# A macaron layer on one Trainium2 core: another order of work in the mixer, mean squares by wide products, inverse roots by log, exp and a Newton step

## The chip, the cores and the metric

The kernel runs on one core of a Trainium2 chip. The metric is device microseconds of one execution; the number for a kernel is the median of its runs. A profile is one further execution with every instruction and DMA recorded. Engines are named as in the profile: PE is TensorE (PEld its weight loads), DVE is VectorE, ACT is ScalarE, POOL is GpSimd and SP is SyncE, which issues most DMAs.

## The reference

One layer of a streaming encoder on x (512 tokens by 1024 features, float32):

```
x = x + 0.5 * swiglu(rms(x), ffn1)          # 1024 -> 2816 -> 1024
h = rms(x);  q, k, v, u = h @ w_in          # 512 columns each
a = attention(rms(q), rms(k), v)            # 8 heads of 64, a bias by clipped distance
p = for each window 2, 4, 8, 16: (trailing mean of u - u) @ pool_w * pool_scale
x = x + concat(a, p) @ w_out
x = x + 0.5 * swiglu(rms(x), ffn2)
x = rms(x)
```

rms divides by the square root of the mean square plus 1e-6 and multiplies by a gain. q and k are normed for each token and head.

## The kernel before, in words

All large products are float32 at full precision, made from three products of a high and a low part: `mm3` (L198, L199, L200) issues high by high, low by high or high by low, and the last of the three, each 128 by 128 by 512 or by 256. The parts of a weight are made on the way: SP loads 512 KB, ACT casts the high part (L132, in the mixer L1117), DVE subtracts for the low part (L133, in the mixer L1122). `mm3` reads its moving operand in an order that alternates between the two halves of the row (`p (a i) -> p i a`, a = 2), and the engines that read a PSUM tile put it back with the views `ordered` and `natural`.

The two feed-forward blocks (roughly the first 335 us and the last 310 us of the span) use a seven-product scheme of block sums. POOL makes the sums of the down weights in DRAM: `Down.make_sums` copies one element of a tile named after it (`mark`, so that POOL waits for it) and then issues DMAs that copy or add whole weight rows (L715, L717). For the second block half of those 48 steps are issued in the mixer, as jobs `for i in range(LATE, LATE + EARLY)`: one job for each of the weight chunks 12 to 19, which holds that chunk's buffer until POOL has read it. The other half follows inside the second up-projection.

The three norms `n1`, `n2`, `n3` work with features on partitions, so the mean over features runs across partitions. ACT squares, DVE adds the squares of the eight feature tiles into `acc`. Then, in `per_token` (L319, for n2 L1151), four float32 products of `acc` with a column of ones give a sum per token; ACT takes the root and loads another function table; DVE makes the inverse root with a reciprocal and one Newton step (`rsqrt_of`) and a diagonal block; PE multiplies a block of ones with the diagonals (`spread`, L340, for n2 L1182: one float32 product of 512 columns), so that the value of each token stands on all partitions; ACT copies this to `rb` (L342). In a feed-forward block the first four PSUM banks can't be reused before DVE has read them with `rb` (L424).

The mixer (about 335 to 490 us) is a list of jobs, each with an engine, a cost, a rank and the buffers that it takes and frees. `plan()` orders them on paper, always taking the job of least rank whose inputs and buffers are ready on its own clock, and the instructions are recorded in that order; each engine then runs its list in order. The weight chunks are 4 for the first half of q and k, 4 for v, 4 for the second half, 4 for u, then 8 of the output projection. For each half of q and k: `evacuate` scales the projected tile by the norm `r` on ACT (L1312), ACT squares it (L1318), DVE reduces, `inverse` makes 32 inverse roots per token on DVE alone with an integer first guess and three Newton steps, DVE scales, PE transposes (L1356), ACT and DVE split the result (L1263, L1267). For each pair of heads PE makes the scores (L1516, 64 rows for each head, two heads at once in the two halves of the array); DVE adds the bias and takes the largest (L1524); ACT takes exp (L1532) and divides by the sum (L1543). For each head PE transposes the probabilities (L1580), ACT and DVE split them (L1589, L1594), `multiply` takes the product with v (L1605, 8 products of 512, 512, 384, 384, 128, 128, 256 and 256 columns), and ACT and DVE split its result (L1612, L1615, L1621). The four pooling groups run beside it, sums on POOL (L1430), and end in the map products (operands `m,wp`). The output products follow, then `add_out` on x (L1670).

Of the kernel before, what the change touches and what calls it, by code (L numbers as in the profile page):

```python
# [8 lines left out]
F32 = mybir.dt.float32  # L9
# [22 lines left out]
MAGIC = 1597463007.0  # L32
# [7 lines left out]
EARLY = 8  # L40
LATE = 12
# [4 lines left out]
    weights=(-1.0, 0.905, 3.0), qk=2.0, turn=1.015, head=0.9, pool=0.965, map=3.0, u=0.99,  # L46
    score=0.99, evac=0.3, bias=1.2, wp=1.5, add=0.935, next=0.965,
)
HOP = 0.45
SLOW = dict(act=1.06, dve=1.06)  # L50
# [6 lines left out]
def layer(  # L57
# [162 lines left out]
    ones = const.tile([P, P], F32, name="ones")  # L220
# [3 lines left out]
    nc.vector.memset(eps, EPS)  # L224

    def tables(func, after):

        nc.scalar.activation(table, after, func, scale=0.0)


    tables(AF.Sqrt, ones[:, 0:1])
    idle = abank()
    for _ in range(8):
        nc.tensor.matmul(idle[:, :P], ones, ones, start=True, stop=True)
# [29 lines left out]

    def rsqrt(v, n):

        half = small.tile([P, n], F32, tag=f"rs{n}", name=name("half"), bufs=4)
        y = small.tile([P, n], F32, tag=f"rs{n}", name=name("y"), bufs=4)
        nc.vector.tensor_scalar(
            half.bitcast(I32), v.bitcast(I32), 1, None, op0=ALU.logical_shift_right  # L270
        )
        nc.vector.tensor_scalar(
            y.bitcast(I32), half.bitcast(I32), -1.0, MAGIC, op0=ALU.mult, op1=ALU.add
        )
        for _ in range(3):
            a = small.tile([P, n], F32, tag=f"rs{n}", name=name("a"), bufs=4)
            b = small.tile([P, n], F32, tag=f"rs{n}", name=name("b"), bufs=4)
            z = small.tile([P, n], F32, tag=f"rs{n}", name=name("z"), bufs=4)
            nc.vector.tensor_tensor(a, y, y, op=ALU.mult)
            nc.vector.scalar_tensor_tensor(b, a, -0.5, v, op0=ALU.mult, op1=ALU.mult)  # L280
            nc.vector.scalar_tensor_tensor(z, b, 1.5, y, op0=ALU.add, op1=ALU.mult)
            y = z
        return y
# [10 lines left out]
    class Norm:  # L294
# [22 lines left out]
        def per_token(self, total, after=None):  # L317
            for t in range(NT):
                nc.tensor.matmul(  # L319
                    total[:, t : t + 1], self.acc[:, t * P : (t + 1) * P], ones[:, 0:1],  # L320
                    start=True, stop=True,
                )
            v, root, self.r = (
                small.tile([P, NT], F32, tag=what, name=name(what)) for what in ("v", "root", "r")
            )
            nc.scalar.activation(root, total[:, :NT], AF.Sqrt, scale=1.0 / D, bias=eps)
            if after:
                tables(after, root[:, 0:1])
            nc.vector.tensor_scalar(v, total[:, :NT], 1.0 / D, EPS, op0=ALU.mult, op1=ALU.add)
            rsqrt_of(v, root, self.r)  # L330
            self.diag = temp()
            nc.vector.tensor_tensor(
                self.diag.rearrange("p (t c) -> p t c", t=NT),
                ident.unsqueeze(1).to_broadcast([P, NT, P]),
                self.r.unsqueeze(2).to_broadcast([P, NT, P]),
                op=ALU.mult,
            )

        def spread(self, wide):
            nc.tensor.matmul(wide, ones, self.diag, start=True, stop=True)  # L340
            self.rb = small.tile([P, S], F32, tag="rb", name=name("rb"), bufs=1)
            nc.scalar.copy(self.rb, wide)  # L342

        def finish(self):
            self.per_token(abank(), AF.Silu)
            self.spread(abank())
# [309 lines left out]
    class Down:  # L656
# [14 lines left out]
        def __init__(self, order, pair, block, by_token, ahead=0):  # L671
# [11 lines left out]
            self.steps = sorted(  # L683
                (g + at + 2 * (i - T1), at, i, g)
                for i in self.terms for g in range(G) for at in range(2)
            )
# [124 lines left out]
        def product(self, acc, g, a, i, further=False, scale=None):  # L811
# [7 lines left out]
            if self.n_products == 12:  # L819
                tables(AF.Sqrt, a[0][:, 0, 0:1].bitcast(F32))  # L820
# [120 lines left out]
    with tc.tile_pool(name="mix", bufs=1, reuse_waits="tile") as mpool:  # L941
# [60 lines left out]
        def plan():  # L1002
# [30 lines left out]
            while len(order) < len(jobs):  # L1033
                moved = False
                for e in free:
# [97 lines left out]
        for i in range(LATE, LATE + EARLY):  # L1133
            job(
                "pool", 3.8, 5, lambda i=i: down2.make_sums(buf["part", i][0].bitcast(F32)),
# [13 lines left out]
        def per_token():  # L1149
            for t in range(NT):  # L1150
                nc.tensor.matmul(  # L1151
                    buf["total"][:, t : t + 1], n2.acc[:, t * P : (t + 1) * P], ones[:, 0:1],
                    start=True, stop=True,
                )

        n2_small = {}

        def root_of():
            for what in ("v", "root", "r"):
                n2_small[what] = small.tile([P, NT], F32, tag=what, name=name(what))  # L1160
            nc.scalar.activation(
# [885 lines left out]
```

## Time and profile before

| what | value |
|---|---|
| median of 3 runs | 810.72 us (810.51 to 812.14) |
| the profiled execution's own time | 809.87 us |
| its span, first to last instruction | 808.1 us |
| granted TensorE clock, mean | 0.998 |
| PE busy | 798.1 us (99%) |
| DVE busy | 712.2 us (88%) |
| ACT busy | 499.1 us (62%) |
| POOL busy | 144.8 us (18%) |
| moved by DMA | 158.56 MB, 196 GB/s |
| function tables loaded by ACT (L228) | 7, mean 1283 ns |

Busy time is the share in which an engine has an instruction in work. The ends of matmuls are modelled, so a full PE can hold small gaps; these show as the distance between the starts of two matmuls, which is what the prediction reads. A row of a timeline gives the start, the length, the engine, the line, the operation, out<-in with the tile's names, and shapes; in brackets stands the idle time before it and what ended that. A row of the waits gives who waited for whom, the sum, how often, and the longest. A row of the windows gives the busy time and count of each engine in that stretch, then the granted clock, the DMA share and GB/s.

### The profile page before, as it was taken

The numbers are of one execution on the slowest core, as the hardware profiler recorded it, in microseconds if no ns is written. First come the engines' busy times: TensorE is split into PE (matmuls) and PEld (weight loads), VectorE is DVE, ScalarE is ACT, GpSimd is POOL, SyncE is SP. The second block draws the span as 40 slices with busy tenths as digits, with TensorE's granted clock in tenths as the row PEclk, the third lists the DMA queues.
The fourth block names the chain that finished last, engine by engine and source line by source line (L and its number), as shares of the span: only waits on it lengthen the run. The fifth ranks groups of instructions, "written<-read, shape, count | busy, mean of one in ns | idle before, by whom it ended". The sixth has DMA issues, their size and how long they took to land.

```text
span 808.1 us, 14963 instructions
## 1 busy us (share of the span) xinstructions
PE 798.1 (99%) x5730; PEld 749.4 (93%) x5730; DVE 712.2 (88%) x1136; ACT 499.1 (62%) x854; POOL 144.8 (18%) x232
## 2 busy tenths in 40 slices
PE   9999999999999999999999999999999999999996
PEld 8889999999999999888888888899999999988986
DVE  7899999999996997778688798999989999996997
ACT  8446665556675765559649644465566665766584
POOL 0022222223220000100355354111111011100010
PEclk9999999999999999999999999999999999999999
DMA  8266889979999674431599767256766665869642
GB/s 291 74 209 209 235 226 248 205 194 253 249 291 313 218 215 159 133 119 50 146 256 247 192 209 198 85 116 193 181 175 171 169 182 148 254 238 329 218 143 105
DMA packets 73847, 158.56 MB, mean 196 GB/s; under 512 B 6560, under 2 KB 31664, under 8 KB 73392
## 3 DMA queue, kind: packets, MB, share of 16 engines
q1 hardware_dynamic: 49808, 109.09, 39.8%
q0 software_dynamic: 23680, 48.24, 28.4%
q8 instruction: 45, 0.74, 0.4%
q10 hardware_dynamic: 288, 0.27, 0.1%
q14 instruction: 26, 0.21, 0.1%
HBM read 153.38 MB, written 50.34 MB: 252 GB/s over the span
## 4 chain that ended last, share of the span: by engine, by line
PE 91%; DVE 4%; ACT 1%; issue 1%; ACTq 0%
PE mm L198 19%; PE mm L200 19%; PE mm L199 19%; PE a L199 10%; PE a L198 10%; PE a L200 10%; PE mm L1605 1%; PE mm L1516 1%; DVE aside L365 1%; PE a L1580 1%; PE mm L1580 1%; DVE aside L371 0%; PE a L1516 0%; DVE parts L133 0%; PE a L1605 0%
## 5 line engine op out<-in xcount | busy, mean ns | idle before, releaser
L571 ACT ACTIVATE t<-mm 128x256 f32<-128x256 f32 x105 | 40.5, 385 | 111.0 <-PE mm L200 109.1
L132 ACT CAST parts<-raw 128x1024 fp32r<-128x1024 f32 (+2 forms) x77 | 74.0, 968 | 54.8 <-PE mm L199 24.7
L133 DVE TENSOR_TENSOR parts<-raw,parts 128x1024 fp32r<-128x1024 f32 (+2 forms) x77 | 85.7, 1121 | 15.1 <-ACT parts L132 14.6
L199 PE MATMUL mm<-ha,parts 128*128 128x256 f32 x280 | 77.0, 275 | 0.0
L200 PE MATMUL mm<-ha,parts 128*128 128x256 f32 x280 | 77.0, 275 | 0.0
L198 PE MATMUL mm<-ha,parts 128*128 128x256 f32 x280 | 77.0, 275 | 0.0
L717 POOL DMA_DIRECT2D wsum<-in_wB_dram x72 | 71.0, 1123 | 26.0 <-DMA wsum<-wsum 14.2
L715 POOL COPY mark<-t 128x1 f32<-128x1 f32 x40 | 16.1, 403 | 331.0 <-DVE t L615 245.0
L482 DVE TENSOR_TENSOR parts<-wsum,parts 128x1024 fp32r<-128x1024 f32 x53 | 64.5, 1217 | 5.1 <-ACT parts L477 5.1
L477 ACT CAST parts<-wsum 128x1024 fp32r<-128x1024 f32 x53 | 53.8, 1047 | 0.7 <-PE mm L200 0.3
L198 PEld LDWEIGHTS mm<-ha,parts 128*128 128x128 f32 x280 | 53.8, 192 | 0.1
L199 PEld LDWEIGHTS mm<-ha,parts 128*128 128x128 f32 x280 | 53.8, 192 | 0.1
L200 PEld LDWEIGHTS mm<-ha,parts 128*128 128x128 f32 x280 | 53.8, 192 | 0.0
L198 PE MATMUL mm<-hhi,parts 128*128 128x512 f32 x128 | 49.5, 391 | 0.1
L200 PE MATMUL mm<-hhi,parts 128*128 128x512 f32 x128 | 48.7, 384 | 0.8 <-DVE parts L133 0.8
L133 DVE TENSOR_TENSOR ah<-acts,ah 128x512 fp32r<-128x512 f32 (+1 forms) x72 | 47.1, 661 | 2.6 <-ACT ah L132 2.5
L199 PE MATMUL mm<-hlo,parts 128*128 128x512 f32 x128 | 48.7, 382 | 0.0
L132 ACT CAST ah<-acts 128x512 fp32r<-128x512 f32 (+1 forms) x72 | 40.9, 580 | 8.8 <-PE mm L199 6.2
L482 DVE TENSOR_TENSOR parts<-raw,parts 128x512 fp32r<-128x512 f32 (+1 forms) x52 | 43.5, 857 | 0.6 <-ACT parts L477 0.6
L500 DVE TENSOR_TENSOR wsum<-raw 128x1024 f32<-128x1024 f32 x35 | 42.6, 1217 | 0.0
L477 ACT CAST parts<-raw 128x512 fp32r<-128x512 f32 (+1 forms) x52 | 39.3, 755 | 4.0 <-DMA raw<-in_wA_dram 3.5
L1122 DVE TENSOR_TENSOR parts<-raw,parts 128x1024 fp32r<-128x1024 f32 x24 | 30.3, 1265 | 11.4 <-ACT parts L1117 11.4
(344 smaller groups left out, 3059.8 us busy)
## 6 DMA issues: line engine op xcount, KB each, us to landing
raw<-in_wA_dram SPq DMA_DIRECT2D x87, 512.0 KB, 5.1
wsum<-in_wB_dram POOLq DMA_DIRECT2D x60, 512.0 KB, 7.4
raw<-wsum SPq DMA_DIRECT2D x36, 512.0 KB, 4.8
raw<-in_wB_dram SPq DMA_DIRECT2D x30, 512.0 KB, 4.8
wsum<-wsum POOLq DMA_DIRECT2D x20, 512.0 KB, 5.1
x<-in_xT_dram SPq DMA_DIRECT2D x16, 256.0 KB, 6.1
raw<-in_wQK_dram SPq DMA_DIRECT2D x8, 512.0 KB, 3.5
wsum<-in_wB_dram POOLq DMA_DIRECT2D x12, 256.0 KB, 5.4
```

What stands on the lines that cost most here:

```text
L132: nc.scalar.copy(hi, src)
L133: nc.vector.tensor_tensor(lo, src, hi.bitcast(F32), op=ALU.subtract)
L198: nc.tensor.matmul(acc, a[0], high, start=start, stop=False, **more)
L199: nc.tensor.matmul(acc, a[0], low, start=False, stop=False, **more)
L200: nc.tensor.matmul(acc, a[1], high, start=False, stop=stop, **more)
L477: nc.scalar.copy(hi, src)
L482: nc.vector.tensor_tensor(lo, src, hi.bitcast(F32), op=ALU.subtract)
L500: nc.vector.tensor_tensor(z, raw[:, : 2 * S], raw[:, S : 3 * S], op=ALU.add)
L571: nc.scalar.activation(natural(dst), ordered(src), AF.Copy, scale=scale)
L717: nc.gpsimd.dma_start(self.rows(i, g), self.rows(self.terms[i][at], g), **(dict(accum_op=ALU.add) if at else {}),)
L1122: nc.vector.tensor_tensor(lo, buf["raw", i], hi.bitcast(F32), op=ALU.subtract)
L1580: nc.tensor.transpose(buf["tp", h, group][:, n : n + P], buf["p", h, t][:, j * P : (j + 1) * P], ident,)
```

## The change

It has four parts.

**Norms.** The block of ones becomes a block of 1/1024. `acc` is multiplied by it in one wide product, so the mean stands on all partitions at once: for n1 and n3 as one float32 product of 512 columns, for n2 as two products on a high and a low part that ACT and DVE make first. ACT then takes log, exp with scale -0.5, and a square (`rough`), all from one function table, and DVE does one Newton step in two passes over 512 columns (`exact`). The four products with a column, the spread and its copy go. For n2, `r` per token is picked out of `rb` with the identity and a reduction. The inverse roots of q and k take log and exp on ACT (32 values each) and three passes on DVE in place of the integer guess and nine passes. The function tables loaded are 5 in place of 7.

**Product with v.** `multiply` reads its moving operand alternating between the halves of each block of 128 columns, and the three readers of the result go through views that undo this.

**Order in the mixer.** Ranks and costs of the planner change, and with them the order on every engine.

**Sums.** The mixer's 24 steps of weight sums become 16 jobs on chunks 4 to 19, and their sequence is by kind: first all copies of a kind, then all additions to them.

The diff, cut:

```diff
-EARLY = 8
-LATE = 12
+EARLY = 16
+LATE = 4
...
-    score=0.99, evac=0.3, bias=1.2, wp=1.5, add=0.935, next=0.965,
+    score=0.5, evac=0.3, bias=1.2, wp=1.1, add=1.1, next=0.965,
...
-SLOW = dict(act=1.06, dve=1.06)
+SLOW = dict(act=1.1, dve=1.06)
...
-    nc.vector.memset(ones, 1.0)
+    nc.vector.memset(mean_of.bitcast(F32), 1.0 / D)
...
+        def mean(self, wide, pair):
+            wide = wide.rearrange("p (i a) -> p i a", a=2)
+            for i in range(2):
                 nc.tensor.matmul(
-                    total[:, t : t + 1], self.acc[:, t * P : (t + 1) * P], ones[:, 0:1],
-                    start=True, stop=True,
+                    wide, mean_of, pair[i].rearrange("p (a i) -> p i a", a=2),
+                    start=i == 0, stop=i == 1,
+                )
+        def rough(self, wide, y, y2):
+            nc.scalar.activation(natural(y), ordered(wide), AF.Ln, bias=eps)
+            nc.scalar.activation(y, y, AF.Exp, scale=-0.5, bias=less_ln2)
+            nc.scalar.activation(y2, y, AF.Square, scale=2.0)
+        def exact(self, wide, y, y2):
+            nc.vector.scalar_tensor_tensor(
+                natural(y2), ordered(wide), EPS, natural(y2), op0=ALU.add, op1=ALU.mult
             )
+            self.rb = small.tile([P, S], F32, tag="rb", name=name("rb"), bufs=1)
+            nc.vector.scalar_tensor_tensor(
+                self.rb, y2, 3.0, y, op0=ALU.subtract, op1=ALU.mult, reverse0=True
             )
...
         def finish(self):
-            self.per_token(abank(), AF.Silu)
-            self.spread(abank())
+            wide, y, y2 = abank(), temp(), temp()
+            nc.tensor.matmul(
+                wide.rearrange("p (i a) -> p i a", a=2), mean_of.bitcast(F32),
+                self.acc.rearrange("p (a i) -> p i a", a=2), start=True, stop=True,
+            )
+            self.rough(wide, y, y2)
+            tables(AF.Silu, y[:, 0:1])
+            self.exact(wide, y, y2)
...
+            if ahead:
+                self.steps = [
+                    (0, at, i, g) for i in (T1, T3, T2, T4) for at in range(2) for g in range(G)
+                ]
...
-                        cost, scoring = cost + 0.1 * (score != scoring), score
+                        cost, scoring = cost + 0.2 * (score != scoring), score
...
-                var["rs"] = rsqrt(z.rearrange("p t h -> p (t h)"), NT * 8).rearrange(
+            def rough():
+                nc.scalar.activation(flat("log"), flat("mean"), AF.Ln)
+                nc.scalar.activation(flat("y"), flat("log"), AF.Exp, scale=-0.5)
...
             def multiply():
-                o = buf["o", h]
+                o = buf["o", h].rearrange("p (b i a) -> p b i a", a=2, i=P // 2)
...
-                            o[:, j * P :], v[j][:, h, :, :],
-                            buf["pT", h, group][i][:, at : at + (NT - j) * P],
+                            o[:, j:], v[j][:, h, :, :],
+                            turned.rearrange("p (b a i) -> p b i a", a=2, i=P // 2),
...
-        job("act", 1.5, 6, lambda: tables(AF.Sqrt, ones[:, 0:1]), list(at_prob.values()))
```

Three places show how the order moves. The first is PE in the first feed-forward block, where the last feature tiles meet the first four banks; `acc` is the sum of squares, `hhi` and `hlo` are the parts of the scaled x. Before:

```order
L199 MATMUL mm_167<-hlo_275,parts 128x512
L319 MATMUL a_330<-ones,acc_191 128x1 x4
L200 MATMUL mm_167<-hhi_274,parts 128x512
L198 MATMUL mm_164<-hhi_309,whi_314 128x512
L199 MATMUL mm_164<-hlo_310,whi_314 128x512
L200 MATMUL mm_164<-hhi_309,wlo_315 128x512
```

And in the changed kernel:

```order
L199 MATMUL mm_172<-hlo_280,parts 128x512
L334 MATMUL a_335<-acc_196,mean_of 128x512
L200 MATMUL mm_172<-hhi_279,parts 128x512
L198 MATMUL mm_169<-hhi_314,whi_319 128x512
L199 MATMUL mm_169<-hlo_315,whi_319 128x512
L200 MATMUL mm_169<-hhi_314,wlo_320 128x512
```

One product of 512 columns stands where four of one column stood, and the spread, which stood 17 products further on, has no successor.

The second place is ACT around the first transposes of q and k: `t` are the projected and the squared tiles, `qk_sb` marks the split of the transposed ones, `prob` the exp of the scores. Before:

```order
L1312 ACTIVATE t_4473<-mm_4306,r_4390 128x512
L1318 ACTIVATE t_4480<-t_4473 128x512
L1117 CAST parts<-raw_4437 128x1024
L1117 CAST parts<-raw_4449 128x1024
L1263 ACTIVATE m_4574<-a_4559,qk_sb 128x512
L1263 ACTIVATE m_4584<-mm_4564,qk_sb 128x512
L1263 ACTIVATE m_4591<-mm_4569,qk_sb 128x512
L1263 ACTIVATE m_4598<-mm_4579,qk_sb 128x512
L1117 CAST parts<-raw_4541 128x1024
L1532 ACTIVATE prob_620_4636,sm_4637<-prob_620_4636,sm_4637 128x512
```

And in the changed kernel:

```order
L1311 ACTIVATE t_4496<-t_4471 128x512
L1116 CAST parts<-raw_4417 128x1024
L1116 CAST parts<-raw_4463 128x1024
L1340 ACTIVATE log_4521<-var_4510 128x32
L1341 ACTIVATE y_4522<-log_4521 128x32
L1116 CAST parts<-raw_4537 128x1024
L1256 ACTIVATE m_4593<-mm_4577,qk_sb 128x512
L1256 ACTIVATE m_4601<-mm_4582,qk_sb 128x512
L1256 ACTIVATE m_4608<-mm_4588,qk_sb 128x512
L1256 ACTIVATE m_4623<-mm_4596,qk_sb 128x512
L1116 CAST parts<-raw_4548 128x1024
L1544 ACTIVATE prob_607_4645,sm_4646<-prob_607_4645,sm_4646 128x512
```

Log and exp of the head norms stand behind two weight casts, and a third cast now stands ahead of the splits.

The third place is PE near the end of the heads: `prob` marks transposes of the probabilities, `pTw` the product with v, `m,wp` the map products, other `m` the output products. Before:

```order
L1580 MATMUL a_5672<-ident,prob_779_5407 128x128
L198 MATMUL mm_5683<-m_5604,wp_4378 128x512
L199 MATMUL mm_5683<-m_5605,wp_4378 128x512
L200 MATMUL mm_5683<-m_5604,wp_4379 128x512
L198 MATMUL mm_5697<-m_5611,wp_4378 128x512
L199 MATMUL mm_5697<-m_5612,wp_4378 128x512
L200 MATMUL mm_5697<-m_5611,wp_4379 128x512
L1580 MATMUL a_5705<-ident,prob_804_5510 128x128
L1580 MATMUL a_5705<-ident,prob_799_5486 128x128
L1605 MATMUL a_5717<-pTw_5691,v_4748 128x512
```

And in the changed kernel:

```order
L198 MATMUL mm_5620<-m_5704,parts 128x512
L199 MATMUL mm_5620<-m_5705,parts 128x512
L200 MATMUL mm_5620<-m_5704,parts 128x512
L1592 MATMUL a_5783<-ident,prob_787_5492 128x128
L1592 MATMUL a_5783<-ident,prob_782_5482 128x128
L198 MATMUL mm_5695<-m_5704,parts 128x512
L199 MATMUL mm_5695<-m_5705,parts 128x512
L200 MATMUL mm_5695<-m_5704,parts 128x512
L198 MATMUL a_5789<-m_5750,wp_4374 128x512
L199 MATMUL a_5789<-m_5751,wp_4374 128x512
L200 MATMUL a_5789<-m_5750,wp_4375 128x512
L1592 MATMUL mm_5797<-ident,prob_790_5510 128x128
```

Map products and transposes that stood back to back now have output products between them. Between the second set of transposes of q and k and the last product with v, PE has 132 products of 512 columns of projection, map and output in place of 102; behind the last product with v stand 129 in place of 150. In the whole mixer the scores stand in 8 separate runs in place of 7.

More of the change, by code (lines that the diff above doesn't have):

```diff
@@ L262, in extended @@
         return load, fill, store
[L265 to L283, printed above, removed]
     def rsqrt_of(v, root, out):
@@ L682, in __init__ @@
             self.loaded, self.then, self.made = {}, {}, []
[L683 to L686, printed above, removed]
+            if ahead:
+                self.steps = [
+                    (0, at, i, g) for i in (T1, T3, T2, T4) for at in range(2) for g in range(G)
+                ]
+            else:
+                self.steps = sorted(
+                    (g + at + 2 * (i - T1), at, i, g)
+                    for i in self.terms for g in range(G) for at in range(2)
+                )
             n = len(self.steps)
@@ L1146, in layer @@
             at_acc = job("dve", 0.65, -5, None, [sq, at_acc])
[L1149 to L1161, printed above, removed]
-                n2_small["root"], buf["total"][:, :NT], AF.Sqrt, scale=1.0 / D, bias=eps
-            )
-            tables(AF.Exp, n2_small["root"][:, 0:1])
@@ L1166, in reciprocal_root, with mean_high, mean_low @@
-        def reciprocal_root():
-            v, n2.r = n2_small["v"], n2_small["r"]
-            nc.vector.tensor_scalar(
-                v, buf["total"][:, :NT], 1.0 / D, EPS, op0=ALU.mult, op1=ALU.add
-            )
-            rsqrt_of(v, n2_small["root"], n2.r)
+        def mean_high():
+            nc.scalar.copy(buf["sum", 0], n2.acc)
+        def mean_low():
+            nc.vector.tensor_tensor(
+                buf["sum", 1], n2.acc, buf["sum", 0].bitcast(F32), op=ALU.subtract
+            )
@@ L1177, in diagonal @@
-                n2.r.unsqueeze(2).to_broadcast([P, NT, P]),
+                by_token(buf["y"]), by_token(n2.rb), ident.unsqueeze(1).to_broadcast([P, NT, P]),
                 op=ALU.mult,
             )
-        def spread():
-            nc.tensor.matmul(buf["wide"], ones, buf["diag"], start=True, stop=True)
-        def spread_copy():
-            n2.rb = small.tile([P, S], F32, tag="rb", name=name("rb"), bufs=1)
-            nc.scalar.copy(n2.rb, buf["wide"])
-        total = z = job("pe", 0.5, -1, per_token, [at_acc], [("bank", "total")])
@@ L1189, in layer, with reduced @@
-        z = job("act", 1.8, -1, root_of, [z])
-        at_r = job("dve", 0.8, -1, reciprocal_root, [z], uses=["total"])
-        z = job("dve", 0.65, -1, diagonal, [at_r], [("t", "diag")])
-        z = job("pe", 0.9, -1, spread, [z], [("bank", "wide")], ["diag"])
-        at_rb = job("act", 0.55, -1, spread_copy, [z], uses=["wide"])
+        def reduced():
+            n2.r = small.tile([P, NT], F32, name="r")
+            nc.vector.tensor_reduce(n2.r, by_token(buf["y"]), axis=AX.X, op=ALU.add)
@@ new lines, in layer @@
+        pair = [("sum", i) for i in range(2)]
+        z = job("act", 0.6, -1, mean_high, [at_acc], [("m", key) for key in pair])
+        z = job("dve", 0.65, -1, mean_low, [z])
+        total = z = job("pe", 0.45, -1, mean, [z], [("bank", "mean")], pair)
+        z = job("act", 1.8, -1, rough, [z], [("t", "y"), ("t", "y2")])
+        z = at_rb = job("dve", 1.3, -1, exact, [z], uses=["mean", "y2"])
+        z = job("dve", 0.65, -1, diagonal, [z])
+        at_r = job("dve", 0.65, -1, reduced, [z], uses=["y"])
@@ L1621, in out_low @@
                 nc.vector.tensor_tensor(
-                    buf[pair[1]][rows, :], buf["rest", h][rows, :], buf["o", h][HD:, :], op=ALU.add
+                    by_block(buf[pair[1]]), by_block(buf["rest", h]), result(1), op=ALU.add
                 )
```

86 lines of the change are left out of this document (51 added, 35 removed).

## The prediction

> **What bounds the kernel now.** I read the page first: engine totals and the chain that ended last.
>
> ```profile
> span 808.1 us, 14963 instructions
> PE 798.1 (99%) x5730; PEld 749.4 (93%) x5730; DVE 712.2 (88%) x1136; ACT 499.1 (62%) x854; POOL 144.8 (18%) x232
> PE 91%; DVE 4%; ACT 1%; issue 1%; ACTq 0%
> ```
>
> PE has something in work for all but 10 us of the span and carries 91% of the chain. So a microsecond is won only by taking work from PE, by making a product shorter, or by closing one of PE's gaps. The second view is the list of PE's waits: who held it, then sum, count and longest in microseconds.
>
> ```profile
> PE a L234 <- DVE eps L224: 1.1, 1, 1.1
> PE mm L200 <- DVE parts L133: 0.8, 1, 0.8
> PE mm L198 <- DVE m L1621: 0.6, 1, 0.6
> PE a L319 <- DVE acc L315: 0.4, 1, 0.4
> PE a L1605 <- DVE pTw L1594: 0.3, 1, 0.3
> ```
>
> The first is the start of the program and stays. The others lie in the first norm and in the mixer, where the change works. All come from DVE, so the third view is the windows around them: stretch, its length, then busy time (count) of PE, PEld, DVE, ACT, POOL, then clock, DMA share and GB/s.
>
> ```profile
> 26.00:52.00 26.00, 25.47 (x117) 21.56 (x115) 23.90 (x32) 10.36 (x13) 3.62 (x4) 1.00 0.26 87
> 425.00:440.00 15.00, 14.97 (x93) 13.09 (x90) 13.21 (x46) 15.00 (x42) 10.84 (x16) 1.00 0.98 230
> 440.00:450.00 10.00, 8.98 (x51) 7.00 (x50) 9.50 (x22) 9.15 (x23) 2.15 (x3) 1.00 0.50 163
> ```
>
> After the first norm DVE works 23.90 of 26 us and then makes PE wait. In the later heads ACT is busy for all 15 us of a stretch, and in the next 10 us PE has its largest hole of the mixer, 1.02 us. The granted clock is 1.00 throughout.
>
> **The change part by part.** For the rate of a product I take a run of full-precision products, and the second norm that follows it.
>
> ```profile
> 340.05 0.38 PE L200 MATMUL mm<-parts,hlo 128*128 128x512 f32 x1
> ...
> 341.99 0.38 PE L200 MATMUL mm<-parts,hlo 128*128 128x512 f32 x1
> 342.21 1.02 PE L1182 MATMUL a<-t,ones 128*128 128x512 f32 x2
> 342.67 0.78 PE L198 MATMUL mm<-parts,hhi 128*128 128x512 f32 x1
> 343.28 0.38 PE L199 MATMUL mm<-parts,hhi 128*128 128x512 f32 x1
> ```
>
> From 340.05 to 341.99 are nine products, 0.2155 us each; lengths overlap, so I count from start to start. From 342.21 to 343.28 stand the spread and one such product: 1.07 - 0.2155 = 0.86 us for a wide float32 product.
>
> The first norm (a row's bracket is the idle time before it, and what ended it):
>
> ```profile
> 21.83 1.05 PE L319 MATMUL a<-ones,acc 128*128 128x1 f32 x8 [0.40 <-DVE acc L315]
> 22.74 0.46 PE L200 MATMUL mm<-hhi,parts 128*128 128x512 f32 x1
> ...
> 27.55 0.59 ACT L342 COPY rb<-a 128x512 f32<-128x512 f32 x1 [2.86 <-PE a L340]
> 28.17 0.69 DVE L424 TENSOR_TENSOR t<-mm,rb 128x512 f32<-128x512 f32 x1 [2.10 <-ACT rb L342]
> ...
> 52.23 0.70 PE L200 MATMUL mm<-hhi,parts 128*128 128x512 f32 x2 [0.75 <-DVE parts L133]
> ```
>
> 1. *First norm.* The column products take 22.74 - 21.83 = 0.91 us and go; the spread, 0.86, is replaced by one product like it. That is -0.9. Then the way to `rb`: before, DVE takes up the first bank at 28.17, 5.4 us after the columns, having idled 2.10. Now follow three ACT passes of 512 elements and two on DVE. With the groups of ACT by form:
>
> ```profile
> L314 ACT ACTIVATE t<-x 128x512 f32<-128x512 f32 x14 | 8.1, 614 | 0.0
> L228 ACT ACT_TABLE_LOAD x7 | 9.0, 1283 | 1.3 <-PEq L2032 1.2
> ```
>
> At 0.61 for an ACT pass and 0.69 for a DVE pass that is 3 x 0.61 + 2 x 0.69 = 3.2 us, and 1.0 for the product (the length at 342.21): 4.2 after 21.83, so about 26.1 instead of 28.17. The 2.10 us in which DVE idled is the only idle time of any size in its 26:52 stretch, and the 0.75 us of PE at 52.23 is its late result. DVE gains about 2 and adds 1.4 us of passes but drops the small steps of the root; with 0.75 needed, I take the wait as gone. Together -1.7. Bounds: 0 if DVE is as late as before by as much as PE is now early, -2.1 if the 0.40 at 21.83 goes too.
>
> 2. *Second norm.* Columns 0.91 and spread 0.86 become two products on parts, 2 x 0.2155 = 0.43: -1.3. The parts cost ACT and DVE a pass each; this lies beside the projection, which does not need `r` until it is read out. If that cover failed, 1.3 would be lost again (0.61 + 0.69).
>
> 3. *Third norm.*
>
> ```profile
> 509.14 1.22 DVE L371 TENSOR_TENSOR aside<-aside 128x1024 f32<-128x1024 f32 x1
> 510.28 0.68 DVE L424 TENSOR_TENSOR t<-mm,rb 128x512 f32<-128x512 f32 x1
> 511.11 0.45 PE L198 MATMUL mm<-hhi,parts 128*128 128x512 f32 x1
> ```
>
> Again -0.9 of columns. But PE starts on the freed bank at 511.11, 0.83 after DVE began to read it (0.68 long): PE follows DVE here, and arriving 0.9 earlier it would wait. In the new order the read stands one pass of 1.22 earlier on DVE. I take half, -0.5; ends 0 and -0.9.
>
> 4. *Product with v, and the scores.*
>
> ```profile
> 360.79 0.38 PE L200 MATMUL a<-parts,hlo 128*128 128x512 f32 x1
> 361.10 0.50 PE L1516 MATMUL a<-m,m 64*128 64x512 f32 x1
> ...
> 361.99 0.48 PE L198 MATMUL mm<-parts,hhi 128*128 128x512 f32 x1
> 362.31 0.38 PE L199 MATMUL mm<-parts,hhi 128*128 128x512 f32 x1
> ...
> 379.90 1.15 PE L1605 MATMUL mm<-pTw,v 128*128 128x512 f32 x6
> ...
> 381.18 0.38 PE L198 MATMUL a<-parts,hhi 128*128 128x512 f32 x1
> ```
>
> One head's eight products have 2560 columns and take 381.18 - 379.90 = 1.28 us; at 0.2155 for 512 they would take 1.08. The full-precision products already read alternating between two halves and are the faster ones per column. If the read order were all of it, 8 heads gain 8 x 0.20 = 1.6; if none, 0. Part of the 0.20 must be the short products of 128 and 256 columns and their many changes of width, so I take -0.6. [...]
>
> A run of scores costs a switch on either side: 361.10 - 360.79 = 0.31 and 362.31 - 361.99 = 0.32 in place of 0.2155, 0.2 together. Eight runs in place of seven: +0.2. Runs and transposes among more products switch more often too; with one such switch I take +0.4, ends +0.2 and +0.5.
>
> 5. *PE's waits in the mixer.*
>
> ```profile
> 443.32 0.60 PE L1580 MATMUL a<-ident,prob 128*128 128x128 f32 x4
> 443.99 0.45 PE L198 MATMUL mm<-m,wp 128*128 128x512 f32 x1
> ...
> 445.43 0.46 PE L198 MATMUL mm<-m,wp 128*128 128x512 f32 x1 [0.56 <-DVE m L1621]
> ...
> 446.24 0.44 PE L1580 MATMUL a<-ident,prob 128*128 128x128 f32 x2
> 446.99 1.25 PE L1605 MATMUL a<-pTw,v 128*128 128x512 f32 x6 [0.32 <-DVE pTw L1594]
> ```
>
> From 443.32 to 446.99, 3.67 us, PE does six transposes of 128 columns and six map products: 6 x 0.2155 = 1.3, and about 0.5 for the transposes (0.3 at the same rate by columns, more for their switches), so about 1.85 is lost. It waits for DVE because map products and transposes stand close together. The new order puts output products between them: 30 more products of 512 columns (6.5 us) before the last product with v. I take two thirds, -1.2; ends +0.5 (the largest single wait here moves elsewhere) and -1.9.
>
> 6. *At nothing.* Two table loads of 1.28 us go from ACT, which PE does not wait for by the list. Log and exp of the head norms add ACT passes of 32 elements and take six from DVE; PE does projections meanwhile. If that cover is gone, that is the third rival. The sums are spread over 16 chunks on POOL, 18% busy, and hold a chunk's buffer longer; no wait of PE is on POOL.
>
> Sum: -1.7 - 1.3 - 0.5 - 0.6 + 0.4 - 1.2 = -4.9. The profiled execution took 809.87, so it would take 805.0; the median of the runs is 810.72, 0.85 above it. I forecast for the median 810.72 - 4.9 = **805.8**. About 0.2%, 1.6 us, is what a measurement of this kernel can tell from no change.
>
> **The rivals.** *DVE stays the bound after both norms* (13%). Where DVE is 92% busy, PE's saved columns turn into a longer wait at the same bank. For: PE already waits for DVE at 52.23 and follows it at 511.11. Against: the 2.10 us hole that DVE has before 28.17. Terms 1 and 3 go: -4.9 + 2.2 = -2.7, 808.0.
>
> *The order does not do what it is there for* (10%). The heads end when ACT ends, and ACT was busy 15.00 of 15 us; moving products cannot help, and the read order gains nothing. Terms 5 and the -0.6 go: -3.1, 807.6. Against it: in 440:450 ACT has 0.85 us to spare, and PE's named releaser is DVE.
>
> *ACT in order, slower* (7%). On ACT the weight casts wait for PE to free a buffer, and everything behind them waits too.
>
> ```profile
> 352.33 1.05 ACT L1117 CAST parts<-raw 128x1024 fp32r<-128x1024 f32 x1 [2.89 <-PE mm L200]
> ...
> 357.30 0.69 ACT L1263 ACTIVATE m<-a,qk_sb 128x512 fp32r<-128x512 f32 x1 [3.92 <-PE a L1356]
> ```
>
> Now log and exp of the head norms stand behind two such casts, and a further cast ahead of the first exps. If each half of q and k comes 2.89 + 1.05 = 3.9 us later and PE finds nothing else, 7.9 us stand against -3.7 (the sum without term 5): 814.9. It decides from the point at which about half of the 7.9 reaches PE. Against: ACT idled 3.92 us before the splits at 357.30, so it has that much room in the first half.
>
> *The alternating read is slow* (3%). If neighbouring reads 64 columns apart cost the products with v as much again, 8 x 1.28 = 10.2 stands where -0.6 did: 810.72 - 4.3 + 10.2 = 816.6. [...] Against: the alternating products take 0.42 ns a column, the straight ones 0.50.
>
> **How the numbers follow.** Forecast 67%, rivals 13, 10, 7 and 3. The forecast's own terms by their ends reach from -7.6 to -0.3; that all go one way is unlikely, so I take about two microseconds below and, where the second and third cases lie, over three above: 803.6 to 809.2. That leaves out the slow cases and a tail on either side. Faster by over 0.2% means below 809.1: the forecast, less some 4%, and the next two cases, 0.86; within 0.2%: 0.05; slower: the last two, less a little of the third, 0.09.
>
> **What would show it.** Right: the norm product of the first norm directly followed by products 0.2155 apart; DVE taking up the first bank near 26 with little idle time; no wait of PE near 51; a head's products with v near 1.2 us; PE's waits in the mixer under 1 us in sum; PE busy about 793. Wrong: idle time of ACT ahead of the first splits that ends with PE, and PE waiting for ACT at the transposes of q and k; a head's products at 1.28 or over; a new wait of PE on DVE in the first four banks of either feed-forward block; PE waiting for POOL's sums or a weight cast where chunks are held longer.

## The result, and the profile after

The changed kernel takes 804.54 us (median of 6 runs, 803.98 to 804.97) against 810.36 us for the kernel before (809.85 to 812.14). The ratio is 0.9925, with a 95% interval of 0.9913 to 0.9937: 0.75% faster. The forecast was 805.8. Its profiled execution took 804.50 us, 5.37 less than that of before; the forecast's sum was -4.9.

The page of the changed kernel: span, busy time of each engine, and the chain that ended last.

```profile
span 802.7 us, 14916 instructions
PE 793.5 (99%) x5706; PEld 745.4 (93%) x5706; DVE 709.3 (88%) x1112; ACT 499.7 (62%) x857; POOL 152.5 (19%) x240
PE 89%; DVE 5%; issue 1%; DMA 1%; ACT 1%; SPq 0%; DVEq 0%; ACTq 0%
```

Of the 5.4 us that the span lost, PE's busy time lost 4.6. The list of PE's waits in the changed kernel:

```profile
PE a L242 <- DVE less_ln L226: 1.1, 1, 1.1
PE mm L200 <- DVE parts L133: 0.5, 1, 0.5
PE a L334 <- DVE acc L305: 0.4, 1, 0.4
PE mm L198 <- DVE t L418: 0.3, 1, 0.3
PE mm L198 <- ACT hhi L135: 0.2, 1, 0.2
```

The waits of the mixer are gone from the list. The one behind the first norm has shrunk from 0.8 to 0.5, and one at the first bank of the second feed-forward block (`t`, L418) is new. The windows show the same (stretch, length, then PE, PEld, DVE, ACT, POOL, clock, DMA share, GB/s); the change moved the mixer's work by 2.6 to 5.3 us, so they are not quite the same work as before:

```profile
26.00:52.00 26.00, 25.51 (x118) 21.97 (x118) 25.93 (x36) 10.38 (x14) 6.10 (x6) 1.00 0.25 89
...
425.00:440.00 15.00, 15.00 (x86) 13.41 (x85) 13.71 (x37) 13.30 (x33) 7.86 (x10) 1.00 0.27 38
440.00:450.00 10.00, 10.00 (x52) 8.78 (x51) 8.49 (x18) 8.34 (x19) 4.12 (x5) 1.00 0.90 205
```

PE is full from 425 to 450 us, and ACT is no longer full in the first of those stretches. DVE now works 25.93 of the 26 us behind the first norm.

To see where the time went, I count the full-precision products (L198 to L200) in both traces in order of their starts. Each kernel makes 5412 of them, so the k-th marks the same progress wherever the work around it is the same:

| product | place | before, us | after, us | difference |
|---|---|---|---|---|
| 70 | ahead of the first norm's product | 21.05 | 21.07 | +0.02 |
| 100 | behind its spread of before | 29.94 | 29.28 | -0.66 |
| 200 | behind the first bank wait | 52.55 | 51.63 | -0.92 |
| 600 | first feed-forward block | 102.04 | 100.63 | -1.41 |
| 2640 | its end | 334.84 | 333.53 | -1.31 |
| 2700 | behind the second norm's product | 349.54 | 346.91 | -2.63 |
| 3180 | end of the mixer | 488.34 | 483.09 | -5.25 |
| 3220 | behind the third norm's product | 498.89 | 493.12 | -5.77 |
| 3400 | behind the first bank waits | 535.20 | 529.80 | -5.41 |
| 5400 | end | 800.14 | 794.74 | -5.40 |

So the first norm gave 1.41, the second 1.32, the mixer 2.62, the third norm 0.16, and 0.1 was lost in between. Of the first norm's 1.41, 0.27 lie near 93 us and in the trace of before alone: two further runs with its lists up to the mixer (`b_newranks` and `b_ranks_sums` below) do not have them. The change at the first norm is worth about 1.15.

The first norm on PE, and then on DVE, in the changed kernel:

```profile
21.84 1.34 PE L334 MATMUL a<-acc,mean_of 128*128 128x512 f32 x2 [0.39 <-DVE acc L305]
22.51 0.89 PE L200 MATMUL mm<-hhi,parts 128*128 128x512 f32 x1
23.24 0.38 PE L198 MATMUL mm<-hhi,whi 128*128 128x512 f32 x1
```

```profile
25.36 0.69 DVE L324 SCALAR_TENSOR_TENSOR t<-a,t 128x512 f32<-128x512 f32 x1 [0.64 <-ACT t L320]
26.09 0.69 DVE L328 SCALAR_TENSOR_TENSOR rb<-t,t 128x512 f32<-128x512 f32 x1
26.82 0.75 DVE L359 SCALAR_TENSOR_TENSOR aside<-x,gain_sb,rb 128x512 f32<-128x512 f32 x1
27.48 0.68 DVE L418 TENSOR_TENSOR t<-mm,rb 128x512 f32<-128x512 f32 x1
```

From 21.84 to 23.24 stand the norm's product and one other: 1.40 - 0.2155 = 1.18 us for it, and not 0.86. The first of DVE's passes on `rb` comes at 26.82, where it came at 28.17.

The third norm, DVE and PE at the first bank:

```profile
494.18 0.68 DVE L328 SCALAR_TENSOR_TENSOR rb<-t,t 128x512 f32<-128x512 f32 x1
494.89 2.74 DVE L359 SCALAR_TENSOR_TENSOR aside<-x,gain_sb,rb 128x512 f32<-128x512 f32 x4
...
504.87 0.68 DVE L418 TENSOR_TENSOR t<-mm,rb 128x512 f32<-128x512 f32 x1
```

```profile
505.70 0.45 PE L198 MATMUL mm<-hhi,parts 128*128 128x512 f32 x1 [0.33 <-DVE t L418]
```

PE starts 0.83 behind DVE's read, as it did before (511.11 - 510.28): it follows DVE here, and of the 0.52 that its own work had saved by product 3220, 0.36 went into the wait.

### The profile page after: what moved, and what is told of

It reads as the page before. It is cut to its first block, busy times and chain, and to the rows that moved or that the text cites. A ratio compares the mean times of both kernels' runs of the same rounds, so it can differ in the third digit from the quotient of the medians.

```text
span 802.7 us, 14916 instructions
## 1 busy us (share of the span) xinstructions
PE 793.5 (99%) x5706; PEld 745.4 (93%) x5706; DVE 709.3 (88%) x1112; ACT 499.7 (62%) x857; POOL 152.5 (19%) x240
## 4 chain that ended last, share of the span: by engine, by line
PE 89%; DVE 5%; issue 1%; DMA 1%; ACT 1%; SPq 0%; DVEq 0%; ACTq 0%
PE mm L200 18%; PE mm L198 18%; PE mm L199 18%; PE a L198 11%; PE a L199 11%; PE a L200 10%; DVE aside L359 1%; PE mm L1528 1%; DVE parts L133 1%; PE mm L1592 1%; DMA raw<-in_wA_dram 1%; DVE aside L365 1%; PE a L1618 1%; PE mm L1618 1%; PE a L1592 0%
## 5 line engine op out<-in xcount | busy, mean ns | idle before, releaser
L200 PE MATMUL mm<-ha,parts 128*128 128x256 f32 x280 | 77.0, 275 | 0.0
L198 PE MATMUL mm<-ha,parts 128*128 128x256 f32 x280 | 77.0, 275 | 0.0
L198 PEld LDWEIGHTS mm<-ha,parts 128*128 128x128 f32 x280 | 53.8, 192 | 0.1
L200 PEld LDWEIGHTS mm<-ha,parts 128*128 128x128 f32 x280 | 53.8, 192 | 0.0
L200 PE MATMUL mm<-hhi,parts 128*128 128x512 f32 x120 | 45.9, 385 | 0.5 <-DVE parts L133 0.5
L198 PE MATMUL mm<-hhi,parts 128*128 128x512 f32 x120 | 45.4, 382 | 0.7 <-DVE t L418 0.3
L199 PE MATMUL mm<-hlo,parts 128*128 128x512 f32 x120 | 46.0, 385 | 0.0
L1116 ACT CAST parts<-raw 128x1024 fp32r<-128x1024 f32 x24 | 25.1, 1046 | 25.8 <-DMA raw<-in_wQK_dram 6.0
```

Source lines behind the costliest of these rows:

```text
L198: nc.tensor.matmul(acc, a[0], high, start=start, stop=False, **more)
L199: nc.tensor.matmul(acc, a[0], low, start=False, stop=False, **more)
L200: nc.tensor.matmul(acc, a[1], high, start=False, stop=stop, **more)
L1116: return lambda: nc.scalar.copy(buf["part", i][0], buf["raw", i])
```

## The experiments

Times are medians with the ratio to the kernel before, run beside it on the same chip; in brackets stands the 95% interval. The first 20 us (weights arriving) and places near 93, 206 and 741 us differ by 0.3 to 0.7 us between executions of like code, and the bank wait of the third norm by up to 0.2 us between runs whose lists on PE, DVE and ACT are the same. So a stretch of a trace is measured by the count of products from its start to its end, against the changed kernel's trace unless said.

**The planner's numbers undone** (`a_oldranks`).

```diff
-    ... turn=1.1, head=0.9, pool=0.965, map=0.95, u=2.0, score=0.5, wp=1.1, add=1.1
+    ... turn=1.015, head=0.9, pool=0.965, map=3.0, u=0.99, score=0.99, wp=1.5, add=0.935
-SLOW = dict(act=1.1, dve=1.06)
+SLOW = dict(act=1.06, dve=1.06)
-                        cost, scoring = cost + 0.2 * (score != scoring), score
+                        cost, scoring = cost + 0.1 * (score != scoring), score
```

> The changed kernel with the planner's ranks and costs of before; norms, reads and sums stay as changed. Theory A (the new order alone took PE's waits out of the mixer): the waits of about 2.2 us at the end of the heads come back, less 0.2 for one run of scores fewer, so 806.5, between 805.9 and 807.2, and the trace shows PE waiting for DVE where transposes and map products meet. Theory B (the waits went because the products with v and the head norms became shorter, whatever the order): 804.5 within 0.4, with no such wait.

It took 807.10 us, ratio 0.9962 (0.9950 to 0.9974). The mixer is 1.43 us longer, and a wait is back in PE's list:

```profile
PE a L1592 <- ACT prob L1555: 1.0, 1, 1.0
```

The order is worth 1.4 us with the new sums, less than the 2 of theory A, and PE waits for ACT there, not DVE. The rest of the median's 2.6 us lies, in the profiled execution, at the start (0.63), near 741 us (0.45) and at the third norm (0.21). The scores stand in 8 runs here too, not in one fewer as I had expected.

**The weight sums undone** (`a_oldsums`). The lists of PE, ACT, DVE and SP stay word for word.

```diff
-EARLY = 16
-LATE = 4
+EARLY = 8
+LATE = 12
...
-            if ahead:
-                self.steps = [
-                    (0, at, i, g) for i in (T1, T3, T2, T4) for at in range(2) for g in range(G)
-                ]
+            self.steps = sorted(
+                (g + at + 2 * (i - T1), at, i, g)
+                for i in self.terms for g in range(G) for at in range(2)
+            )
...
-                "pool", 2.0, 5, lambda i=i: down2.make_sums(buf["part", i][0].bitcast(F32)),
+                "pool", 3.8, 5, lambda i=i: down2.make_sums(buf["part", i][0].bitcast(F32)),
```

> The changed kernel with the sums of the down weights as before: 8 jobs on chunks 12 to 19, old sequence of steps. Only POOL's list differs. Theory A (POOL's spread sums are hidden): 804.5 within 0.4, and PE's waits in the mixer and in the second feed-forward block unchanged. Theory C (the spread sums keep chunks, DMA or DVE free where heads end, and that is why PE's waits there went): about 2 us slower, 806.5.

808.89 us, 0.9984 (0.9975 to 0.9994): most of the gain is gone. The mixer is 3.9 us longer. POOL, then DVE, then PE in this run:

```profile
407.59 0.51 POOL L711 DMA_DIRECT2D wsum<-wsum  x1 [6.25 <-DMA wsum<-in_wB_dram]
...
417.01 0.50 POOL L711 DMA_DIRECT2D wsum<-wsum  x1 [6.82 <-DMA wsum<-in_wB_dram]
...
418.81 1.07 POOL L1437 TENSOR_TENSOR us<-u 128x527 f32<-128x527 f32 x1
```

```profile
423.53 0.69 DVE L1445 SCALAR_TENSOR_TENSOR t<-us,u 128x512 f32<-128x512 f32 x1 [1.56 <-POOL us L1437]
433.93 0.69 DVE L1445 SCALAR_TENSOR_TENSOR t<-us,u 128x512 f32<-128x512 f32 x1 [4.99 <-POOL us L1437]
```

```profile
435.68 0.44 PE L1587 MATMUL a<-ident,prob 128*128 128x128 f32 x2 [1.33 <-ACT prob L1550]
438.38 0.81 PE L1613 MATMUL a<-pTw,v 128*128 128x512 f32 x3 [0.75 <-DVE pTw L1601]
```

POOL issues an addition only when the copy that it adds to has landed, and stands still 6.25 and 6.82 us ahead of these two. The sums of a pooling group are behind it in POOL's list; DVE's subtraction waits up to 4.99 us for them; the softmax of the heads is behind that on DVE; ACT and PE wait in turn. PE's list names, in the mixer, ACT and DVE only: the cause is three engines back. In the trace of before POOL has the same waits from 340 to 490 us:

```profile
POOL wsum L717 <- DMA wsum<-in_wB_dram: 19.4, 5, 6.6
```

Yet DVE waits nowhere for POOL there from 395 to 460 us, because that order reaches the pooling groups later: DVE's first two subtractions start at 425.82 and 432.56, in the changed kernel at 421.66 and 427.16. So theory C holds in direction, at twice its size; the way over POOL's list was not in it.

**Which half of the sums** (`a_oldsteps`, `a_oldchunks`). The first takes the old sequence alone, the second the old chunks (and job cost) alone; the edits are the middle part and the outer parts of the diff above.

> The changed kernel with 16 jobs on chunks 4 to 19, but the weight sums in their old sequence, in which an addition soon follows the copy that it adds to. Only POOL's list differs. Theory H (in the old sequence POOL waits for a copy to land before it can issue the addition, the sums of the pooling groups stand behind that on POOL, and DVE and the heads behind those): POOL again waits several times about 6 us for its own DMAs, DVE waits for the sums of the pooling groups, and the mixer is 2 to 4 us longer, 806.5 to 808.5. Rival I (what costs is to have all 24 steps on the last eight chunks): 804.5 to 805.2.

> The changed kernel with the new sequence of the weight sums (copies first, then additions), but in 8 jobs on chunks 12 to 19 as before. Only POOL's list differs. Theory H: no addition waits long for a copy, so the pooling groups' sums come in time and the mixer is at most 0.8 us longer: 804.5 to 805.3. Rival I: 2 to 4 us longer, as with the old sums whole.

804.96 us, 0.9936 (0.9922 to 0.9950), and 805.21 us, 0.9935 (0.9921 to 0.9949). The mixer's length changes by 0.0 and by +0.47. Theory H falls as stated, and so does rival I: neither half alone costs much, and in neither does POOL wait for a copy from 340 to 490 us. Only additions close behind their copies and packed into eight chunks make the 3.9 us.

**Ranks alone, and ranks with sums, on the kernel before** (`b_newranks`, `b_ranks_sums`). The edits are those above, the other way round.

> The kernel before with the new ranks and costs of the planner alone; norms, reads and sums as before. Theory A (the order alone takes PE's waits out of the mixer): -1.6 to -2.2 against before, 808.2 to 808.8. Rival G (the new order works only together with the shorter norms or products): -0.5 or less, 809.9 or over, with waits left beside the transposes.

> The kernel before with the new ranks and costs and the new weight sums; norms and read of the product with v as before. It differs from the run with new ranks alone in POOL's list only. Theory J (the mixer's gain needs order and sums together, and nothing else): PE's waits of about 2.2 us in the mixer go, +0.2 for a run of scores more: -1.6 to -2.2 against before, 808.0 to 808.7. Rival G (it also needs the shorter norms or products): -1 or less, 809.2 or over.

With ranks alone 811.14 us, ratio 1.0012 (1.0002 to 1.0022); against before its mixer is only 0.6 us shorter, and its third norm 0.75 longer. With the sums too 809.38 us, 0.9985 (0.9976 to 0.9995), and its mixer is 2.4 us shorter. By their times both runs lie where rival G has them, but in the mixer theory J holds: order and sums together take out the waits, without the other parts. I had expected a run of scores more; both have 6 runs, one fewer than before, so at the prediction's 0.2 for a run about 2.2 of the 2.4 come from waits.

Between these two runs only POOL's list differs, and the old sums cost 1.8 us. But DVE waits for POOL only once, 0.88 us: here the price comes mainly by another way. ACT and DVE with ranks alone:

```profile
419.55 1.05 ACT L1117 CAST parts<-raw 128x1024 fp32r<-128x1024 f32 x1 [1.81 <-DMA raw<-in_wO_dram]
420.64 1.50 DVE L1122 TENSOR_TENSOR parts<-raw,parts 128x1024 fp32r<-128x1024 f32 x1 [1.86 <-ACT parts L1117]
```

A weight chunk lands late while POOL's transfers run: the DMA share from 410 to 420 us is 0.89, with the new sums 0.51, and there the same cast does not wait. DVE's work on the scores stands behind this chunk, and PE's scores after 422.4 take 1.09 longer. The other 0.74 is at a product with v near 460.5, behind a cast that waits 2.52 us for its chunk in place of 1.56. That the late chunks cause the two losses is read from the traces and was not tried by itself.

Of the time of the run with ranks and sums 2.8 us went back at the third norm, 2.2 of it by a rival that I had not named. ACT and then PE there:

```profile
493.04 1.04 ACT L132 CAST parts<-raw 128x1024 fp32r<-128x1024 f32 x1 [4.20 <-DMA raw<-in_wA_dram]
```

```profile
494.13 0.48 PE L198 MATMUL mm<-hhi,parts 128*128 128x512 f32 x1 [1.07 <-ACT parts L132]
```

The first weights of the second feed-forward block came late for the earlier end of the mixer. In the changed kernel the same cast waits 1.77 us and PE does not. This profiled execution is the slowest of the run's ten (810.95 us, median 809.38), so the lateness need not be in every one.

**The read of the product with v undone** (`a_oldpv`).

```diff
-                            o[:, j:], v[j][:, h, :, :],
-                            turned.rearrange("p (b a i) -> p b i a", a=2, i=P // 2),
+                            o[:, j * P :], v[j][:, h, :, :],
+                            buf["pT", h, group][i][:, at : at + (NT - j) * P],
```

> The changed kernel with the product with v read straight, as before; every engine's list is the same. Theory A (the gain is the read alone): a head's products take 1.28 us instead of 1.20, eight times 0.08 is 0.62, so 805.2, between 804.8 and 805.6. Theory B (shorter products with v also opened the waits behind them): new waits beside the heads and 806 or more. Theory D (hidden behind other waits): 804.5 within 0.3.

805.35 us, 0.9948 (0.9932 to 0.9964). One head in the changed kernel, and in this run:

```profile
375.80 1.09 PE L1618 MATMUL a<-pTw,v 128*128 128x512 f32 x6
...
377.00 0.38 PE L198 MATMUL mm<-parts,hhi 128*128 128x512 f32 x1
```

```profile
376.05 1.16 PE L1617 MATMUL a<-pTw,v 128*128 128x512 f32 x6
...
377.33 0.38 PE L198 MATMUL mm<-parts,hhi 128*128 128x512 f32 x1
```

1.20 against 1.28 us, and the mixer is 0.54 longer: theory A.

**The head norms' inverse undone** (`a_oldinv`): integer guess and nine passes on DVE, no log and exp on ACT.

```diff
-                nc.scalar.activation(flat("log"), flat("mean"), AF.Ln)
-                nc.scalar.activation(flat("y"), flat("log"), AF.Exp, scale=-0.5)
...
+                var["rs"] = rsqrt(flat("mean"), NT * 8).rearrange("p (t h) -> p t h", h=8)
```

> The changed kernel with the inverse roots of q and k by the integer guess and nine passes on DVE, at the same places of the order; log and exp of the head norms are left out on ACT. Theory A (this part is hidden behind projections): 804.5 within 0.4. Theory B (it is on the way to the first scores, and its saving is part of the mixer's gain): DVE's extra passes of about 0.16 us, eight more in each half, less ACT's two passes, delay the transposes of q and k by about 0.5 us a half and PE waits there: up to 1 us slower, 805.5.

806.08 us, 0.9948 (0.9933 to 0.9963). The mixer is 0.13 us longer, so this part is hidden, as theory A has it, though the median lies above its range (in the trace of before such a pass on 32 values took 0.18 to 0.19 us, not 0.16); the rest of the median's 1.5 us lies at the start (0.51) and near 741 us (0.67) in its profiled execution, and one of its four runs took 804.60.

**The norm product read straight** (`a_straight`), and **the sum of squares in two parts** (`a_pair`), in the first and third norm.

```diff
-                wide.rearrange("p (i a) -> p i a", a=2), mean_of.bitcast(F32),
-                self.acc.rearrange("p (a i) -> p i a", a=2), start=True, stop=True,
+                wide, mean_of.bitcast(F32), self.acc, start=True, stop=True,
```

```diff
+            nc.scalar.copy(hi, self.acc)
+            nc.vector.tensor_tensor(lo, self.acc, hi.bitcast(F32), op=ALU.subtract)
+            self.mean(wide, [hi, lo])
```

> The changed kernel, where the wide norm product of the first and third norm reads the sum of squares straight and not alternating between halves (the views behind it are undone too); every engine's list is the same. In the changed kernel this product takes 1.19 us from start to start, where the spread of before, the same product read straight, took 0.86. Theory E (the alternating read makes a float32 product slower): 0.86 here, so -0.33 at each of the two norms on PE. Theory F (DVE's unbroken work behind rb sets PE's next start): the first norm keeps its 0.33, since rb comes 0.33 earlier too, and the wait near 51 us stays at about 0.5; at the third norm the wait for a bank near 506 us grows by up to 0.33. So 803.9 to 804.2. Rival: the 1.19 us is something else than the read: no difference, 804.5 within 0.2.

> The changed kernel, where the first and third norm take their mean as the second does: ACT and DVE split the sum of squares into two parts and PE makes two products of full rate, 0.43 us instead of 1.19. Theory F (the chain over ACT and DVE to rb, and DVE's work behind it, sets PE's next start): rb comes at least 0.5 us later (0.61 and 0.69 more, 0.75 less), and PE's wait near 51 us grows by what its product saves and by the delay: 805.0 to 805.7. Rival (PE's own work in these norms sets the end): -0.76 twice, 803.0.

Straight: 804.88 us, 0.9939 (0.9925 to 0.9952), which can't be told from the changed kernel. Its first norm:

```profile
22.54 1.13 PE L334 MATMUL a<-acc,mean_of 128*128 128x512 f32 x2 [0.39 <-DVE acc L305]
23.10 0.78 PE L200 MATMUL mm<-hhi,parts 128*128 128x512 f32 x1
23.72 0.38 PE L198 MATMUL mm<-hhi,whi 128*128 128x512 f32 x1
```

23.72 - 22.54 - 0.2155 = 0.96 us, 0.22 less than the alternating read. Why it is still 0.10 more than the spread's 0.86 was not tried. The first norm keeps the 0.22 to product 600, as theories E and F have it, with 0.22 in place of 0.33. At the third, 0.09 of it goes back into the bank wait, which is less than like runs differ there.

In two parts: 806.27 us, 0.9956 (0.9943 to 0.9970). PE's product is 0.75 shorter, and the first norm is 1.76 us longer by product 600. DVE waits longer for ACT's passes on it:

```profile
26.35 0.69 DVE L324 SCALAR_TENSOR_TENSOR t<-a,t 128x512 f32<-128x512 f32 x1 [1.58 <-ACT t L320]
```

PE loses its 0.75 again at once, in waits of 0.40 for the parts and 0.55 for DVE's first bank; up to product 260 the run is only 0.09 behind. The rest comes near 64 us:

```profile
63.85 0.38 PE L198 MATMUL mm<-xa,parts 128*128 128x256 f32 x1 [0.55 <-ACT t L565]
...
65.10 0.38 PE L200 MATMUL mm<-xa,parts 128*128 128x256 f32 x1 [0.76 <-DVE parts L476]
```

So at the first norm the way to `rb` counts and PE's shorter product does not, as theory F has it, but the wait near 51 us did not grow. How much of the 1.67 us near 64 us is the later `rb` and how much the other order on DVE and ACT, which the scheduler also changed, was not tried. The third norm ends with +0.07.

**One more pass on DVE** (`a_twice`), and **no Newton step** (`a_no_newton`), in the same two norms.

```diff
             self.exact(wide, y, y2)
+            nc.vector.scalar_tensor_tensor(
+                self.rb, y2, 3.0, y, op0=ALU.subtract, op1=ALU.mult, reverse0=True
+            )
```

```diff
-            nc.scalar.activation(y, y, AF.Exp, scale=-0.5, bias=less_ln2)
-            nc.scalar.activation(y2, y, AF.Square, scale=2.0)
+            nc.scalar.activation(self.rb, y, AF.Exp, scale=-0.5)
...
-            self.exact(wide, y, y2)
```

> The changed kernel with the last DVE pass of the first and third norm made twice: one more DVE pass of 0.69 us (0.61 from start to start) ahead of the feed-forward work, nothing more on PE. Theory F (DVE's work behind rb sets PE's next start): +0.6 at the first norm, seen as a longer wait of PE near 51 us, and +0.3 to +0.6 at the third near 506 us: 805.4 to 805.7. Rival (PE's own work sets it): 804.5 within 0.2.

> The changed kernel where the first and third norm leave out the Newton step: log and exp give rb at once (one ACT pass and two DVE passes of 512 columns less at each), and their product reads straight. So rb is as exact as ACT's log and exp make it. Theory F (at the first norm the way to rb and DVE's unbroken work behind it set PE's next start): rb 1.5 to 2 us earlier, and PE's wait of 0.5 us near 51 us is gone, with the 0.2 of the product itself: -0.7 to -0.9 there; at the third norm the wait near 506 us shrinks: -0.3 to -0.7. 803.0 to 803.5. Rival (another work than this chain holds DVE at 51 and 506 us): -0.2 to -0.4 from the products alone, 804.1 to 804.3.

One more pass: 806.00 us, 0.9949 (0.9935 to 0.9962). The added pass took 0.69 us and started 0.72 behind the one before it, not 0.61. PE's wait behind the first norm doubles, from 0.49 to

```profile
52.39 0.48 PE L200 MATMUL mm<-hhi,parts 128*128 128x512 f32 x1 [0.97 <-DVE parts L133]
```

and the first norm is 0.58 longer at product 200, 0.85 at 600. The third norm does not change (-0.05), but not because the pass is free there: the scheduler put the bank's read behind one of the passes of 1.2 us (L365 in the changed kernel) in place of two. That brings PE past the bank 0.57 earlier, and 0.52 are lost again by product 3400. No Newton step: 804.55 us, 0.9931 (0.9919 to 0.9944), where 803.0 to 803.5 was expected. The first norm is 0.65 shorter by product 600; the third is 0.40 *longer*. DVE and PE there:

```profile
492.67 4.06 DVE L357 SCALAR_TENSOR_TENSOR aside<-x,gain_sb,rb 128x512 f32<-128x512 f32 x6
...
505.03 0.68 DVE L416 TENSOR_TENSOR t<-mm,rb 128x512 f32<-128x512 f32 x1
```

```profile
505.86 0.45 PE L198 MATMUL mm<-hhi,parts 128*128 128x512 f32 x1 [0.95 <-DVE t L416]
```

DVE began on `rb` 2.2 us earlier (492.67 against 494.89), and yet the read that frees the bank came at 505.03 against 504.87, because the scheduler put more of DVE's other passes ahead of it. So theory F holds at the first norm and falls at the third: there it is the place of that read in DVE's list that counts. No version was clearly faster than the changed kernel; a straight read with the bank's read put earlier on DVE was not tried.

## Why the prediction was right, point by point

**First norm**, -1.7 forecast, -1.41 measured. Right: columns and spread against one product, and the rest from DVE's earlier start, which the added pass and the missing Newton step show. Two sizes were off. "A wide float32 product like it" cost 1.18 and not 0.86 us, of which 0.22 is its alternating read; with the three ACT passes at 0.63 to 0.72, `rb` was ready near 26.8 and not 26.1. And "I take the wait as gone" failed: DVE's idle time of 2.10 shrank to gaps of 0.57 and 0.64 ahead of 25.36, and 0.49 of the 0.75 us at PE stayed. Between products 200 and 600 another 0.49 went that was not forecast: 0.22 near 63 us, and the 0.27 near 93 us that is no effect of the change. Without that 0.27 the term is about 1.15.

**Second norm**, -1.3 forecast, -1.32 measured.

**Third norm**, -0.5 forecast, -0.16 measured, for the reason given: PE follows DVE at the bank. Halving was too kind; the first rival's mechanism holds here for the most part, and the new wait on DVE at the bank is one of the signs of being wrong that the prediction named. Its other half, at the first norm, does not hold.

**Product with v**, -0.6 forecast; 8 x (1.28 - 1.20) = 0.62. That the choice of about a third of the possible 1.6 came out right is luck in the size, since no row gave it; the sign was argued from rows. How much of what a head loses against 0.2155 us for 512 columns lies with short products was not tried: its two products of 256 columns together took 0.29 us before and 0.27 after. The last rival is out: no run shows its "as much again", 10.2 us for the eight heads; the alternating read is the faster one here, 1.20 us a head against 1.28. **Scores**, +0.4 forecast: from start to start the scores take 9.15 us after and 8.93 before, with one more switch about +0.3.

**PE's waits in the mixer**, -1.2 forecast. The mixer's 2.62 are 0.62 from the product with v, -0.3 for the scores, and so, as what is left, 2.3 from waits. The 2.2 of the run with ranks and sums agrees. That is more than my end of -1.9, where I had counted one place (1.85). The step that failed is the reason: not the order alone. With the old sums the changed kernel loses 3.9 us, and on the kernel before the new order alone gains 0.6 in the mixer.

**At nothing.** For the inverse of q and k this holds (0.13). For the sums it failed: "no wait of PE is on POOL" was true of the trace of before and said nothing of the changed kernel's order, in which DVE comes to the pooling groups sooner. The third rival, ACT in order, did not come; PE waits for no weight cast in the mixer. What did threaten was the same mechanism on POOL.

The term that was too small (the waits, by 1.1) and those that were too large (the first and third norm, by 0.6 together) partly cancelled, which is luck; the sum was 0.5 off by the profiled executions. By the medians the kernel gained 5.8 us, 0.9 more than forecast, and 805.8 was 1.3 too high, because the median of before also came out 0.36 lower than the 810.72 it was worked out from.

## What to carry to other kernels

A wait list names the last engine of a chain. Before calling an off-path queue free, look what stands behind its own waits in program order, and who needs that in the *new* order; the price here was 3.9 us with not one row of PE naming POOL. The old sums cost 1.8 us on the kernel before, there, as far as the traces show, mostly by late weight chunks. At the first norm here, behind which DVE works 25.93 of 26 us, the way to the norm's result counted, and a shorter product on PE was worth only what it shortened of that way: a product shorter by 0.22 us kept its 0.22, and one shorter by 0.75, with `rb` later, lost the 0.75 at once in PE's waits.

## What the runs showed of the hardware

Reading a product's moving operand in alternation between two halves went both ways in these runs. For the products with v, whose operands are the rounded float32 parts, alternating between halves of 64 columns took 1.20 us a head against 1.28 straight (`a_oldpv`). For the float32 product of 512 columns, alternating between halves of 256 took 1.18 us against 0.96 straight (`a_straight`). Whether the type, the distance or the width decides was not tried.
